# A two-layer attention and retention trunk: transposed halves joined, rotation read from PSUM, outputs kept in the gate tiles, retention scores multiplied earlier

## The chip, the cores and the metric

One core of a Trainium2 chip runs the whole program. The metric is device time in microseconds (us) of one execution, median of the runs. The engines are TensorE (PE, with its weight loads PEld), VectorE (DVE), ScalarE (ACT), GpSimd (POOL) and SyncE (SP), which here issues all DMAs.

## What is computed

The input x has 2048 tokens of 1024 numbers (f32). Two layers follow, and a last RMS norm. Cut to what matters:

```
h    = rms_norm(x, gain)
proj = h @ w_in                      # 1024 -> 8 x 512: aq ak av ag rq rk rv rg
ya   = softmax(aq ak' / 8 + bias[clipped distance]) av      # 8 heads x 64, own chunk of 64 and 8 before
rq, rk = rotary(rq), rotary(rk) * 128 ** -0.5               # 4 heads x 128
yr   = rms_norm(chunkwise retention of rq, rk, rv)          # decay by distance inside a chunk, a state between
y    = concat[ya * silu(ag), yr * silu(rg)]
x    = x + y @ w_out

def apply_rotary(t, cos, sin):
    t1, t2 = split(t, 2)             # halves of 64
    return concat([t1 * c - t2 * s, t1 * s + t2 * c])
```

## The kernel before

**Numbers in two halves.** Every matrix product is made from f16 pairs: a value is split into an upper f16 (`hi`, made by ACT as a rounding copy) and the rest (`lo`, made by DVE as value minus upper), and three products hi*hi, hi*lo, lo*hi are summed in PSUM. So most tiles come as two, `hTh`/`hTl` (normed rows, transposed, one pair for each block of 512 tokens), `whT`/`wlT` (weights), `rh`/`rl` (rows before they are transposed).

**Groups and blocks.** A layer is cut into four groups s (two attention heads and one retention head each), a group into four blocks n of 512 tokens (`NS`), a block into four token tiles a of 128. For each (layer l, group s, block n) there is
- `dense_T`: four projections, j = 0 to 3 (q, k, rotary q, rotary k), with the features on the partitions: 24 matmuls of 512 columns each into a `psD` tile (two buffers), then `evacuate(j)`;
- `dense_V`: four token tiles a, v, rv and both gates, 24 matmuls each into `psD`; then ACT makes v, the gate's Tanh (into `gt`, five buffers) and rv, and `rests` on DVE the low parts;
- `attention`: eight units (a, hx), each with its scores `S` (one PSUM buffer), the exponential, `pq` (upper and rest of the probabilities), a DMA transposition into `pT`, and two units later the product `o` with v; its output, times gate, goes to `ya` and by DMA to `y_d` in DRAM;
- `retention`: for each tile a the scores r1 = rk rq (three products), masked and split into `dT`, and then r2: dT times rv, the state's halves `sh` times rq, and the state's update; its output goes to `yr` and by DMA to `y_d`.

After the last group `wout` loads `y_d` tile by tile, splits, transposes (`y_turn`) and multiplies by w_out; for layer 0 `residual` norms and transposes the new rows.

**What sets the order.** PE, ACT, DVE and POOL run in program order, as written by `run`: in each round one generator step of the dense work (8 matmuls of 512 columns), then `tick()` (what was put off by `later(k, fn)` and is due), then one step of the attention of the block before, then background work from `pull` (weights of the next group, norms). A block is 24 rounds, 12 of `dense_T` and 12 of `dense_V`; an attention unit is 3 rounds, a token tile 6. In round 0 of a tile `next(ret)` issues r1, in round 5 r2; in the very first block (`slow`) r1 and r2 alternate in round 2 of each unit. `later(1..3)` after r1 mask it (DVE, L875), round it (ACT, L860) and make the rest (DVE, L864). SP's order is left to a planner, but for the first block, where it is written by hand.

**The rotation before** (`evacuate`, j = 2 and 3; L662 to L683). ACT copies the PSUM tile to SBUF (`raw`), two DMAs swap its 64-partition halves into `swp`, and then in later rounds DVE multiplies raw by the cosine table `tabc`, swp by the signed sine table `tabs`, and adds; ACT rounds (`upper`), DVE makes the rest (`lower`), ACT a third part, and for k a DMA transposes both halves into `kt`. For q, ACT and DVE make `qq`, and four DMAs (L638) copy its two heads to both halves of the partitions of `st.q`; for k, four DMAs (L649 to L652) place the halves of `kk`. `qq`, `swp`, `tabc`, `tabs` have one buffer each.

The tables of cosine and sine are made on DVE and ACT in the first group (`tables`), stored in DRAM (`tab_d`) and loaded for each block.

Of the kernel before, what the change touches and what calls it, by code (L numbers as in the profile page):

```python
# [13 lines left out]
ALU = mybir.AluOpType  # L14
# [13 lines left out]
def hybrid_trunk(ctx: ExitStack, tc: tile.TileContext, x, pos, gain, gcol, w_in, w_out, rel, fgain,  # L28
# [41 lines left out]
    tab_d = [dp.tile([2, P, 512], F32, tag=f"tab{n}", name=f"tab{n}") for n in range(NS)]  # L70
# [12 lines left out]
    def tables(n, wk):  # L83

        ang, k, r, k2 = wk
# [38 lines left out]
        dve.tensor_scalar(ang, r, -1.0, None, op0=ALU.mult)  # L124
        yield
        for hf in range(2):
            sl = slice(hf * 64, hf * 64 + 64)
            cs = slice(hf * 256, hf * 256 + 256)
            sp.dma_start(tab_d[n][0, 0:64, cs], k2[sl, :])
            sp.dma_start(tab_d[n][0, 64:128, cs], k2[sl, :])  # L130
            sp.dma_start(tab_d[n][1, 0:64, cs], ang[sl, :])
            sp.dma_start(tab_d[n][1, 64:128, cs], r[sl, :])
# [3 lines left out]
    TAB_STEPS = 19  # L136
# [78 lines left out]
    def hT_of(l, n):  # L215
        if (l, n) not in hT:
            hT[l, n] = (hp.tile([P, KT, 512], F16, tag="hTh", name=f"hTh{l}_{n}"),
                        hp.tile([P, KT, 512], F16, tag="hTl", name=f"hTl{l}_{n}"))
        return hT[l, n]

    def row_pair(nm):
        return (b2.tile([P, 1280], F16, tag="sc", name=f"rh{nm}")[:, 0:D],
                b2.tile([P, 1280], F16, tag="pq", name=f"rl{nm}")[:, 0:D])
# [11 lines left out]
    def transpose_rows(rows, dh, dl):  # L235
        sp.dma_start_transpose(out=dh, in_=rows[0])
        sp.dma_start_transpose(out=dl, in_=rows[1])

    class Tok:


        def __init__(self, t, xt, rows):
            self.t, self.x, self.rows, self.nm = t, xt, rows, f"n0_{t}"
            self.hh, self.hl = (h_[:, :, t % 4 * P:(t % 4 + 1) * P] for h_ in hT_of(0, t // 4))
# [21 lines left out]
        def hi(self):  # L266
            if self.rows:
                self.rw = (self.rows[:, 0:D], self.rows[:, D:2 * D])
                act.activation(self.rw[0], self.x, AF.Copy)
                return  # L270
            for h in range(2):
                act.activation(self.hh[:, h * KT // 2:(h + 1) * KT // 2, :], self.pt[h], AF.Copy)

        def lo(self):
            if self.rows:
                dve.tensor_tensor(self.rw[1], self.x, self.rw[0], op=ALU.subtract)
                return
# [4 lines left out]
        def dma(self):  # L282
            transpose_rows(self.rw, self.hh, self.hl)
# [324 lines left out]
    def dense_T(l, s, n, g, st):  # L608
        hh, hl = hT[l, n]
        nm = f"{l}_{s}_{n}"  # L610
        st.tabc = b1.tile([P, 512], F32, tag="tabc", name=f"tabc{nm}")
        st.tabs = b1.tile([P, 512], F32, tag="tabs", name=f"tabs{nm}")
        def tab_load():
            while n not in tab_done:
                pull(1)
            sp.dma_start(st.tabc, tab_d[n][0])
            sp.dma_start(st.tabs, tab_d[n][1])
# [9 lines left out]
        def evacuate(j, ps):  # L627
            if j == 0:
                st.q = b2.tile([P, 2, 2, 512], F16, tag="q", name=f"q{nm}")
                qq = b1.tile([P, 2, 512], F16, tag="qq", name=f"qq{nm}")  # L630
                act.activation(qq[:, 0, :], ps, AF.Copy, scale=2.0 ** -16)

                def q_rest():
                    dve.scalar_tensor_tensor(out=qq[:, 1, :], in0=ps, scalar=2.0 ** -16, in1=qq[:, 0, :], op0=ALU.mult,
                                             op1=ALU.subtract)
                    for hx in range(2):
                        for half in range(2):
                            sp.dma_start(st.q[half * 64:half * 64 + 64, hx], qq[hx * 64:hx * 64 + 64])  # L638

                soon(q_rest)  # L640
            elif j == 1:
                st.k = b3.tile([P, 2, 512], F16, tag="k", name=f"k{nm}")
                kk = b1.tile([P, 2, 512], F16, tag="swp", name=f"kk{nm}")
                kh, kl = kk[:, 0, :], kk[:, 1, :]
                act.activation(kh, ps, AF.Copy, scale=2.0 ** -16)

                def k_rest():
                    dve.scalar_tensor_tensor(out=kl, in0=ps, scalar=2.0 ** -16, in1=kh, op0=ALU.mult, op1=ALU.subtract)
                    sp.dma_start(st.k[0:64, 0, :], kh[0:64, :])  # L649
                    sp.dma_start(st.k[64:128, 1, :], kh[64:128, :])  # L650
                    sp.dma_start(st.k[64:128, 0, :], kl[0:64, :])
                    sp.dma_start(st.k[0:64, 1, :], kl[64:128, :])  # L652

                soon(k_rest)
            else:
                w = 5 - j
                rot = b2.tile([P, w, 512], F16, tag=f"rot{j}", name=f"rot{nm}_{j}")
                if j == 2:
                    raw = rot[:, 1:3].rearrange("p a c -> p (a c)").bitcast(F32)
                else:  # L660
                    raw = b1.tile([P, 512], F32, tag="qq", name=f"raw{nm}")
                act.activation(raw, ps, AF.Copy, scale=2.0 ** -16)  # L662

                def swap(rot=rot, raw=raw, j=j):
                    swp = b1.tile([P, 512], F32, tag="swp", name=f"swp{nm}_{j}")
                    sp.dma_start(swp[0:64, :], raw[64:128, :])
                    sp.dma_start(swp[64:128, :], raw[0:64, :])

                    def turned(out_, x_, y_, op):
                        return lambda: dve.tensor_tensor(out_, x_, y_, op=op)  # L670

                    def upper():
                        act.activation(rot[:, 0], raw, AF.Copy)

                    def lower():
                        dve.tensor_tensor(rot[:, 1], raw, rot[:, 0], op=ALU.subtract)

                    def third():
                        act.activation(rot[:, 2], rot[:, 0], AF.Copy, scale=2.0 ** -11)

                    def tokens():
                        st.kt = b1.tile([P, KT, P], F16, tag="ktok", name=f"kt{nm}")
                        sp.dma_start_transpose(out=st.kt, in_=rot.rearrange("p a c -> p (a c)"))  # L683
# [5 lines left out]
                    later(d + 3, upper)  # L689
                    later(d + 4, lower)  # L690
                    if j == 2:
                        later(d + 5, third)
                    else:
                        later(d + 5 if first else 11, tokens)

                if j == 2:
                    st.rq = rot
                    swap()
                    if first:
                        later(1, tab_load)  # L700
                else:
                    st.rk = rot
                    later(8 if first else 2, swap)
# [34 lines left out]
    def dense_V(l, s, n, g, st):  # L738
        hh, hl = hT[l, n]
# [38 lines left out]
    def attention(l, s, n, g, st, prev):  # L778
# [4 lines left out]
        ya = {}  # L783

        def qk(a, hx):
# [16 lines left out]
            v = b2.tile([P, 640], F32, tag="sc", name=f"sc{u.nm}")[:, 0:w]  # L802
# [5 lines left out]
            pq = b2.tile([P, 1280], F16, tag="pq", name=f"pq{u.nm}")  # L808
# [6 lines left out]
        def pv(u):  # L815
            t = 4 * n + u.a
# [7 lines left out]
            def out_():  # L824
# [3 lines left out]
                if u.hx == 0:  # L828
                    ya[u.a] = b2.tile([P, P], F32, tag="ya", name=f"ya{u.nm}")
                y = ya[u.a]  # L830
                vs = slice(u.hx * 64, u.hx * 64 + 64)
# [7 lines left out]
        ret = retention(l, s, n, g, st)  # L839
        slow = (l, s, n) == (0, 0, 0)  # L840
# [25 lines left out]
    def retention(l, s, n, g, st):  # L866
        for a in range(4):
# [4 lines left out]
            r1 = psR.tile([P, 512], F32, tag="small", name=f"r1{nm}")  # L872
            products(r1[:, 0:P], [(st.rk[:, i, cs], st.rq[:, j, cs]) for i, j in ((0, 0), (0, 1), (1, 0))])
            dT = b1.tile([P, 2, P], F16, tag="dT", name=f"dT{nm}")
            later(1, lambda r1=r1: dve.tensor_tensor(r1[:, P:2 * P], r1[:, 0:P], g.msk, op=ALU.mult))  # L875
            later(2, lambda dT=dT, r1=r1: upper_of(dT, r1[:, P:2 * P]))
            later(3, lambda dT=dT, r1=r1: rest_of(dT, r1[:, P:2 * P]))
            yield
# [32 lines left out]
            def fin(t=t, a=a, r2=r2, ss=ss, nm=nm):  # L911
                y = b1.tile([P, P], F32, tag="yr", name=f"yr{nm}")
                dve.scalar_tensor_tensor(out=y, in0=r2[:, 0:P], scalar=ss[:, 0:1], in1=st.g[a][:, P:256],
                                         op0=ALU.mult, op1=ALU.mult)
# [582 lines left out]
```

## Time and profile before

| | |
|---|---|
| runs, median (lowest to highest) | 2116.13 us (2115.45 to 2116.34), 3 runs |
| profiled execution, span of its instructions | 2120.7 us, 4.6 above the median of the runs |
| ACT and POOL busy in it | 1136.9 us (54%) and 432.8 us (20%) |
| mean granted TensorE clock | 0.987 |
| mean busy share of the 16 DMA engines | 66.4% for SP's queue |

The profiled execution has no time of its own beside its span. A profile's lines name engine, source line (L731 is line 731 of the kernel), operation and tiles as out<-in. "idle before" is the engine's idle time ahead of such instructions, with what ended it. SPq is SP's queue: its entries are the issuing of DMAs. PE's durations overlap one another, since matmuls are pipelined.

### The profile page before, as it was taken

How to read it: one execution, taken by the hardware profiler on the slowest of the kernel's cores; microseconds unless marked ns; L12 is line 12 of the kernel's file. 1: busy time of each engine (PE TensorE's matmuls, PEld its weight loads, DVE VectorE, ACT ScalarE, POOL GpSimd, SP SyncE). 2: the span in 40 equal slices, each digit the busy share in tenths (PEclk: the TensorE clock that was granted, in tenths of full speed). 3: DMA queues.
4: the chain of work that ended last, by engine and by line, in shares of the span. 5: the costliest groups of instructions: out<-in, count | busy, mean ns of one | idle time of the engine just before them, and what ended most of it. 6: DMA issues, size and time to landing. Idle time of an engine off the chain costs nothing.

```text
span 2120.7 us, 39351 instructions
## 1 busy us (share of the span) xinstructions
PE 2014.2 (95%) x14014; PEld 1052.9 (50%) x14014; DVE 1341.8 (63%) x4031; ACT 1136.9 (54%) x2522; POOL 432.8 (20%) x509
## 2 busy tenths in 40 slices
PE   6788999999999999988999999999999999998998
PEld 4334455555555555444444555555555555554543
DVE  7667666666656666566654666566666566666643
ACT  7455565556565554554544546554655665445432
POOL 1112221222122212221000222222222222222200
PEclk9989999999999999999999999999999999999999
DMA  8757675557476765689865556655666866648864
GB/s 247 173 111 162 138 157 119 115 110 156 109 166 133 157 164 100 120 189 254 219 179 123 119 100 135 130 119 100 140 129 123 172 152 157 124 101 176 217 193 127
DMA packets 645702, 313.63 MB, mean 148 GB/s; under 512 B 459233, under 2 KB 602081, under 8 KB 645505
## 3 DMA queue, kind: packets, MB, share of 16 engines
q1 hardware_dynamic: 645504, 311.12, 66.4%
q8 instruction: 109, 1.79, 0.4%
q14 instruction: 89, 0.72, 0.1%
HBM read 123.26 MB, written 41.98 MB: 78 GB/s over the span
## 4 chain that ended last, share of the span: by engine, by line
PE 50%; DMA 8%; DVE 5%; ACT 5%; issue 1%; SPq 1%; POOL 0%; POOLq 0%; DVEq 0%; ACTq 0%
PE dT L731 16%; PE dV L752 15%; PE dO L1093 12%; DMA pT<-pq 3%; PE r L856 2%; PE S L800 2%; PE S L801 2%; DVE sc L804 1%; DMA toep<-rel_d 1%; DMA swp<-rot 1%; PE o L820 1%; ACT pq L809 1%; PE o L821 1%; PE o L822 1%; ACT sc L807 1%
## 5 line engine op out<-in xcount | busy, mean ns | idle before, releaser
L807 ACT ACTIVATE sc<-sc,mq,cT 128x640 f32<-128x640 f32 (+4 forms) x256 | 218.4, 853 | 657.3 <-DVE mq L806 341.5
L810 POOL TENSOR_TENSOR pq<-sc,pq 128x640 f16<-128x640 f32 (+4 forms) x256 | 322.6, 1260 | 1201.7 <-ACT pq L809 610.3
L731 PE MATMUL dT<-hTh,whT 128*128 128x512 f16 x1008 | 350.2, 383 | 13.4 <-DMA hTh<-hTl 9.8
L752 PE MATMUL dV<-whV,hTh 128*128 128x512 f16 x1024 | 355.3, 383 | 4.1 <-DVE gt L770 4.1
L752 PE MATMUL dV<-wlV,hTh 128*128 128x512 f16 x1024 | 353.8, 381 | 0.0
L752 PE MATMUL dV<-whV,hTl 128*128 128x512 f16 x1024 | 353.7, 381 | 0.0
L731 PE MATMUL dT<-hTh,wlT 128*128 128x512 f16 x1008 | 347.0, 379 | 0.0
L731 PE MATMUL dT<-hTl,whT 128*128 128x512 f16 x1008 | 346.8, 379 | 0.0
L752 PEld LDWEIGHTS <-hTh 128*128 128x128 f16 x2048 | 197.5, 99 | 222.9 <-issue 8.2
L731 PEld LDWEIGHTS <-whT 128*128 128x128 f16 x2016 | 192.9, 98 | 225.8 <-issue 23.1
L804 DVE CUSTOM_DVE_ANT_0 sc<-S,bias 128x640 f32<-128x640 f32 (+4 forms) x256 | 188.6, 737 | 79.9 <-PE S L801 69.0
L1093 PE MATMUL dO<-whO,yhy 128*128 128x512 f16 x512 | 195.0, 381 | 1.1 <-DMA yhy<-rhy 1.1
L1093 PE MATMUL dO<-whO,yly 128*128 128x512 f16 x512 | 194.8, 381 | 1.1 <-DMA yly<-rly 1.1
L1093 PE MATMUL dO<-wlO,yhy 128*128 128x512 f16 x512 | 194.6, 380 | 0.0
L809 ACT ACTIVATE pq<-sc 128x640 f16<-128x640 f32 (+4 forms) x256 | 171.5, 670 | 12.5 <-DMA pT<-pq 4.6
L1093 PEld LDWEIGHTS <-yhy 128*128 128x128 f16 x1024 | 100.0, 98 | 116.7 <-DMA yhy<-rhy 1.9
L752 PEld LDWEIGHTS <-hTl 128*128 128x128 f16 x1024 | 99.5, 98 | 110.5 <-issue 2.6
L731 PEld LDWEIGHTS <-wlT 128*128 128x128 f16 x1008 | 97.6, 98 | 109.0 <-issue 1.8
L800 PE MATMUL S<-k,q 128*128 128x128 f16 (+3 forms) x592 | 143.7, 269 | 5.7 <-DVE mq L804 5.6
L820 PE MATMUL o<-v,pT 128*128 128x65 f16 x1120 | 130.2, 194 | 14.6 <-DMA pT<-pq 14.6
L820 PEld LDWEIGHTS <-pT 128*128 128x128 f16 x1120 | 105.6, 97 | 52.5 <-DMA pT<-pq 24.4
L801 PE MATMUL S<-k,q 128*128 128x128 f16 (+3 forms) x592 | 131.2, 270 | 0.0
(350 smaller groups left out, 3354.4 us busy)
## 6 DMA issues: line engine op xcount, KB each, us to landing
q<-qq SPq DMA_DIRECT2D x128, 128.0 KB, 2.5
yyy<-y_d SPq DMA_DIRECT2D x32, 512.0 KB, 4.6
stT<-in_w_in_dram SPq DMA_DIRECT2D x27, 512.0 KB, 5.0
stV<-in_w_in_dram SPq DMA_DIRECT2D x26, 512.0 KB, 4.5
k<-kk SPq DMA_DIRECT2D x128, 64.0 KB, 2.1
swp<-rot SPq DMA_DIRECT2D x64, 128.0 KB, 2.6
tabc<-tab SPq DMA_DIRECT2D x32, 256.0 KB, 2.7
tabs<-tab SPq DMA_DIRECT2D x32, 256.0 KB, 2.8
```

Of the source, the lines that this page charges most:

```text
L731: pe.matmul(ps, w_[:, j, kt, :], h_[:, kt, :], start=(m == 0), stop=(m == 23))
L752: pe.matmul(ps, h_[:, kt, a * P:(a + 1) * P], w_[:, kt, :], start=(m == 0), stop=(m == 23))
L800: pe.matmul(o, st.q[:, hx, 0, cs], k_, start=True, stop=False)
L801: pe.matmul(o, st.q[:, hx, 1, cs], k_, start=False, stop=True)
L804: dve.tensor_tensor_reduce(out=v, in0=S[:, 0:w], in1=g.bias[hx][:, 640 - w:640], scale=1.0, scalar=-3.0e38, op0=ALU.add, op1=ALU.max, accu ...
L807: act.activation(v, v, AF.Exp, bias=m[:, 0:1], scale=g.c[:, 0:1])
L809: act.activation(pq[:, 0:w], v, AF.Copy)
L810: pool.tensor_tensor(pq[:, w:2 * w], v, pq[:, 0:w], op=ALU.subtract)
L820: pe.matmul(o[:, 0:65], u.p[:, b, :], v_[:, 0:65], start=(b == 0), stop=False)
L821: pe.matmul(o[:, 0:64], u.p[:, b, :], v_[:, 65:129], start=False, stop=False)
L856: pe.matmul(out_, w_, m_, start=(i == 0), stop=(i + 1 == len(pairs)))
L1093: pe.matmul(ps, h_[:, kt, :], w_[:, kt, :], start=(m == 0), stop=(m == 23))
```

## The change

- **Halves together.** `hTh` and `hTl` become one tile, and so do the rows' halves and the transposed y; one DMA transposes 2048 columns where two had 1024 each. `sc` (scores, f32) and `pq` become one tile `spq` of two buffers, since the rows' halves lie there. `tabc`/`tabs` become `tab`, `qq`/`swp` become `qk`.
- **Rotation straight from PSUM.** DVE multiplies PSUM by the cosine into `own`, and by the sine, crossing the halves, into `other`: one operation of 64 partitions for each half, reading one half and writing the other. ACT's copies and the swap DMAs go; the sign sits in the scalar, so the table is stored once. q and k are written by ACT and DVE in place, half by half; k needs no DMA, q one for each head.
- **Outputs in the gate tiles.** The products with the gate are written over the gate; when both heads and the retention of a token tile are done (`finished`), one DMA stores the tile.
- **Scores sooner.** r1 and its mask, rounding and rest move to `decayed`, called in round 4 of the tile before (for a block's first tile: in the last tile of the block before; for a layer's first block, 11 rounds after `dense_V` starts). `slow` goes: r2 is issued in round 5 of every tile.

The core of the diff:

```diff
     def transpose_rows(rows, dst):
-        sp.dma_start_transpose(out=dh, in_=rows[0])
-        sp.dma_start_transpose(out=dl, in_=rows[1])
+        sp.dma_start_transpose(out=dst, in_=rows[2])
...
-                qq = b1.tile([P, 2, 512], F16, tag="qq", name=f"qq{nm}")
-                act.activation(qq[:, 0, :], ps, AF.Copy, scale=2.0 ** -16)
+                for hx in range(2):
+                    hs = slice(hx * 64, hx * 64 + 64)
+                    act.activation(st.q[hs, hx, 0], ps[hs], AF.Copy, scale=2.0 ** -16)
                 def q_rest():
-                    dve.scalar_tensor_tensor(out=qq[:, 1, :], in0=ps, scalar=2.0 ** -16, in1=qq[:, 0, :], op0=ALU.mult,
-                                             op1=ALU.subtract)
                     for hx in range(2):
-                        for half in range(2):
-                            sp.dma_start(st.q[half * 64:half * 64 + 64, hx], qq[hx * 64:hx * 64 + 64])
+                        hs, os = slice(hx * 64, hx * 64 + 64), slice(64 - hx * 64, 128 - hx * 64)
+                        dve.scalar_tensor_tensor(out=st.q[hs, hx, 1], in0=ps[hs], scalar=2.0 ** -16, in1=st.q[hs, hx, 0],
+                                                 op0=ALU.mult, op1=ALU.subtract)
+                        sp.dma_start(st.q[os, hx], st.q[hs, hx])
...
                 def k_rest():
-                    dve.scalar_tensor_tensor(out=kl, in0=ps, scalar=2.0 ** -16, in1=kh, op0=ALU.mult, op1=ALU.subtract)
-                    sp.dma_start(st.k[0:64, 0, :], kh[0:64, :])
-                    sp.dma_start(st.k[64:128, 1, :], kh[64:128, :])
-                    sp.dma_start(st.k[64:128, 0, :], kl[0:64, :])
-                    sp.dma_start(st.k[0:64, 1, :], kl[64:128, :])
+                    for hx in range(2):
+                        hs, os = slice(hx * 64, hx * 64 + 64), slice(64 - hx * 64, 128 - hx * 64)
+                        dve.scalar_tensor_tensor(out=st.k[os, hx], in0=ps[hs], scalar=2.0 ** -16, in1=st.k[hs, hx],
+                                                 op0=ALU.mult, op1=ALU.subtract)
...
-                act.activation(raw, ps, AF.Copy, scale=2.0 ** -16)
-                    sp.dma_start(swp[0:64, :], raw[64:128, :])
-                    sp.dma_start(swp[64:128, :], raw[0:64, :])
-                    d = 5 if j == 2 and first else 3
-                    later(d, turned(raw, raw, st.tabc, ALU.mult))
-                    later(d + 1, turned(swp, swp, st.tabs, ALU.mult))
-                    later(d + 2, turned(raw, raw, swp, ALU.add))
...
+                def cosine():
+                    dve.scalar_tensor_tensor(out=own, in0=ps, scalar=2.0 ** -16, in1=st.tab[:, 0], op0=ALU.mult,
+                                             op1=ALU.mult)
+                def sine(half):
+                    i_, o_ = slice((1 - half) * 64, (2 - half) * 64), slice(half * 64, half * 64 + 64)
+                    dve.scalar_tensor_tensor(out=other[o_], in0=ps[i_], scalar=(half * 2 - 1) * 2.0 ** -16, in1=st.tab[i_, 1],
+                                             op0=ALU.mult, op1=ALU.mult)
+                d = 2 * j if first else 1
+                later(d, cosine)
+                later(d, lambda: sine(0))
+                later(d + 1, lambda: sine(1))
+                later(d + 2, lambda: dve.tensor_tensor(own, own, other, op=ALU.add))
...
+        def finished(a):
+            left[a] -= 1
+            if left[a] == 0:
+                t = 4 * n + a
+                sp.dma_start(y_d[t].rearrange("p (a s c) -> p a s c", a=2, c=P)[:, :, s],
+                             st.g[a].rearrange("p (a c) -> p a c", a=2))
...
-                dve.scalar_tensor_tensor(out=y[:, vs], in0=o[:, 0:64], scalar=rl[:, 0:1], in1=st.g[u.a][:, vs],
-                                         op0=ALU.mult, op1=ALU.mult)
-                if u.hx == 1:
-                    sp.dma_start(y_d[t][:, s * P:(s + 1) * P], y)
+                y = st.g[u.a][:, u.hx * 64:u.hx * 64 + 64]
+                dve.scalar_tensor_tensor(out=y, in0=o[:, 0:64], scalar=rl[:, 0:1], in1=y, op0=ALU.mult, op1=ALU.mult)
+                finished(u.a)
...
             u = qk(a, hx)
-            if i % 2 == 0 and not slow:
-                next(ret, None)
-            yield
-            yield
-            if i % 2 == 1 or slow:
+            yield
+            if hx == 1:
+                if a < 3:
+                    decayed(l, s, n, g, st, a + 1)
+                elif nxt is not None:
+                    decayed(*nxt, 0)
+            yield
+            if hx == 1:
                 next(ret, None)
```

More of the change, by code (lines that the diff above doesn't have):

```diff
@@ L696, in evacuate @@
+                rot = b2.tile([P, 5 - j, 512], F16, tag=f"rot{j}", name=f"rot{nm}_{j}")
                 if j == 2:
                     st.rq = rot
-                    swap()
+                    st.tmp = b1.tile([P, 2, 2, 512], F16, tag="qk", name=f"tmp{nm}")
                     if first:
@@ L871, in retention @@
             last = t == NT - 1
[L872 to L877, printed above, removed]
-            yield
+            dT = st.dT
             r2 = psR.tile([P, 512], F32, tag="small", name=f"r2{nm}")
@@ L1261, in hybrid_trunk @@
     sp.dma_start(invf_sb, invf)
-    t0 = tables(0, [gp.tile([P, 256], F32, tag="gt", name=f"wk{i}") for i in range(4)])
+    t0 = tables(0, b2.tile([P, 2560], F16, tag="spq", name="wk").bitcast(F32)[:, 0:1024])
     go_on(t0)
```

174 lines of the change are left out of this document (85 added, 89 removed).

## Prediction

> **What bounds the kernel now.** I read the page's first two lines, then the busy time by stretch, then the list of what the PE waited for, and last the timeline around the longest waits.
>
> ```profile
> span 2120.7 us, 39351 instructions
> ...
> PE 2014.2 (95%) x14014; PEld 1052.9 (50%) x14014; DVE 1341.8 (63%) x4031; ACT 1136.9 (54%) x2522; POOL 432.8 (20%) x509
> ```
>
> The PE is the bound: 2014.2 of 2120.7 us. The change takes no matmul away, so all that it can win lies in the 106.5 us in which the PE stood still, and in slow clock.
>
> ```profile
> 53.00:106.00 53.00, 40.60 (x201) 18.56 (x198) 34.24 (x88) 25.64 (x52) 6.19 (x13) 0.90 0.75 173
> 106.00:212.00 106.00, 86.03 (x565) 43.35 (x566) 75.32 (x205) 57.59 (x123) 22.46 (x25) 0.90 0.67 137
> ...
> 742.00:848.00 106.00, 106.00 (x767) 56.20 (x766) 67.27 (x204) 53.07 (x127) 23.61 (x27) 1.00 0.59 132
> ```
>
> The columns are stretch, length, busy time of PE, weight load, DVE, ACT and POOL, granted clock, DMA share and GB/s. A settled stretch (742 to 848) has no idle PE at full clock: nothing can be won there. From 53 to 212 us 32.4 us are idle and the clock is 0.90. So the question is which waits end last in the disturbed places.
>
> ```profile
> PE r L856 <- DVE dT L864: 20.5, 16, 5.1
> PE o L820 <- DMA pT<-pq: 14.6, 13, 2.4
> PE r L856 <- ACT dT L860: 10.2, 6, 2.9
> PE dT L731 <- DMA hTh<-hTl: 9.8, 1, 9.8
> PE S L800 <- DVE mq L804: 5.6, 2, 2.9
> ...
> PE dV L752 <- DVE gt L770: 4.1, 5, 1.5
> PE dT L731 <- DMA hTh<-rhn: 3.6, 1, 3.6
> ...
> PE r L856 <- DVE sh L864: 2.9, 3, 1.7
> ```
>
> The largest item (total us, times, longest) is the retention's second product, waiting for the decayed scores dT: 20.5 + 10.2 = 30.7 us. Next come the transposed probabilities (14.6) and the first rows of a new 512-token block (9.8 + 3.6). The timeline shows why dT is late at the longest of these waits:
>
> ```profile
> 102.17 1.26 SPq L236 DMA_TRANSPOSE hTh<-rhn  x1
> ...
> 103.62 0.47 SPq L666 DMA_DIRECT2D swp<-rot  x1
> 104.14 0.59 SPq L667 DMA_DIRECT2D swp<-rot  x1
> ...
> 106.76 0.69 DVE L670 TENSOR_TENSOR rot<-rot,tabc 128x512 f32<-128x512 f32 x1 [2.90 <-DMA swp<-rot]
> ...
> 110.09 0.28 DVE L864 SCALAR_TENSOR_TENSOR dT<-dT,r 128x128 f16<-128x128 f16 x1
> ...
> 110.43 0.29 PE L856 MATMUL r<-rv,dT 128*128 128x128 f16 x1 [5.07 <-DVE dT L864]
> ```
>
> Start and length lead each line. SP issued the swap of the rotary halves only at 103.62, behind a transposition; DVE, which takes its work in order, stood 2.90 us for it; everything queued behind, L864 among it, slid, and the PE stood 5.07 us.
>
> **Part 1, scores two rounds sooner.** In the chain that ended last, two equal places of consecutive blocks of the settled part are 52.08 us apart:
>
> ```profile
> 1196.32 5.18 PE dT L731 x24
> ...
> 1248.40 5.18 PE dT L731 x24
> ```
>
> That is 24 rounds of 2.17 us. Before, the scores are multiplied in round 0 of a tile's six rounds, masked, rounded and rested in the ticks of rounds 1, 2, 3, and used in round 5. After, they are multiplied in round 4 of the tile before: the last step falls in round 1, four rounds (8.7 us) ahead of its use instead of two (4.3). In the first block the distance was three rounds from product to use, with the last step in the very round of its use; there it becomes seven. The longest wait is 5.1 us, so 4.3 us more cover nearly every one. What is next late is sh, the halved state, which keeps its three rounds and now is first in line: 2.9 us stay, and some 3 us more that dT's lateness hid (the two are written by the same engines, sh one round earlier). So of 33.6 us (dT and sh) 28 go. Bounds: 15 if half of DVE's lateness reaches sh too, 33 if sh's goes as well. The PE work (three small products a tile) is moved, not added. ACT's rounding into the one dT buffer now comes one round after the previous tile's use instead of three, so ACT may stand up to a round for the PE; what is queued behind it is the next exponential, whose probabilities are used six rounds after their scores, so I cost this at nothing; without that cover it would be 2.17 us a tile on ACT.
>
> **Part 2, rotation from PSUM.** ACT's two copies a block (L662) and four swap DMAs go; DVE gets the sine product in two halves of 64 partitions, each reading one half of the PSUM tile and writing the other half. For q and k, ACT's rounding and DVE's rest become two halves each. The groups by line:
>
> ```profile
> L670 DVE TENSOR_TENSOR swp<-swp,tabs 128x512 f32<-128x512 f32 x64 | 44.0, 687 | 0.1
> ...
> L648 DVE SCALAR_TENSOR_TENSOR kk<-dT,kk 128x512 f16<-128x512 f32 x32 | 22.1, 689 | 39.3 <-ACT kk L645 39.2
> ...
> L662 ACT ACTIVATE raw<-dT 128x512 f32<-128x512 f32 x32 | 18.8, 588 | 9.1 <-PE dT L731 9.1
> L645 ACT ACTIVATE kk<-dT 128x512 f16<-128x512 f32 x32 | 18.8, 587 | 3.9 <-PE dT L731 3.9
> ```
>
> No row has a half-height operation on 512 columns. One end is that it costs as much as a full one (the columns are the same), the other half of it; I take the first. DVE then has four more operations of 0.69 us a block (two sines, one q, one k): 4 x 0.69 x 32 = 88 us, 1342 to 1430, or 67% of the span; at half price 0. ACT loses 2 x 0.588 and gains 2 x 0.587 a block: nothing, or minus 38 at half price. In the settled stretch DVE would go from 67.3 to about 73 of 106 us: still no bound. Against the added busy time stands blocked time that goes, in the list of waits:
>
> ```profile
> DVE rot L670 <- DMA swp<-rot: 60.1, 26, 6.2
> ...
> DVE raw L670 <- DMA swp<-raw: 7.3, 1, 7.3
> ```
>
> 67 us in which DVE held its queue for a swap. The dense PSUM tile (two buffers) is held one round longer, till the second sine; its next writer comes four rounds after, so the PE doesn't see it. The table must be there two rounds sooner; the list of waits names no wait of DVE for it now, but in the first two blocks, where it is made just before, it may hold DVE a us or two (in the +3 below).
>
> The Trainium skill's page "VectorE: DVE Perf Modes" (Rules for kernel authors) speaks against this part: for many operations on a matmul's output it would copy PSUM to SBUF first, and its cost table has 120 fixed cycles from PSUM against 58. By it the three products that read PSUM would cost some 65 ns more each, an estimate of 12 us of DVE in all. The rows above disagree: 689 ns from PSUM, 687 from SBUF.
>
> **Part 3, the DMA queue.** All DMAs are issued by SP, one after the other. The list of issues (count, KB, us to landing), and one line's instructions:
>
> ```profile
> q<-qq SPq DMA_DIRECT2D x128, 128.0 KB, 2.5
> ...
> k<-kk SPq DMA_DIRECT2D x128, 64.0 KB, 2.1
> ...
> y_d<-yr SPq DMA_DIRECT2D x128, 64.0 KB, 2.1
> y_d<-ya SPq DMA_DIRECT2D x128, 64.0 KB, 2.1
> ...
> L812 SPq DMA_TRANSPOSE pT<-pq x256: 1167/1334/3015, 84.7 to 1990.5; - x128
> ...
> L667 SPq DMA_DIRECT2D swp<-rot x32: 581/588/824, 54.6 to 1896.7; - x32
> ```
>
> (The last two rows: issue time in ns, least, median, most.) 64 q copies, all 128 k copies and 128 swaps go: 320 x 0.588 = 188 us of SP. Half of the 256 output DMAs go. Of the 54 pairs of row transpositions 52 become one each. The issue hardly grows with width (1.17 at least, where the first tile's 256 columns are, 1.33 typically, for 1280), so 2048 columns should take about 1.5: 52 x 1.2 = 62 us. Together 250 us, 12% of the span, not counting outputs and tables. Who gains: the probabilities' transpositions queue behind less. Of 14.6 us I take 5 (none to 12).
>
> For the second block's rows the queue alone is the wait (SP's timeline):
>
> ```profile
> 71.42 0.51 SPq L666 DMA_DIRECT2D swp<-raw  x1
> 71.97 0.59 SPq L667 DMA_DIRECT2D swp<-raw  x1
> 72.67 1.56 SPq L236 DMA_TRANSPOSE hTh<-hTl  x1
> 74.32 3.10 SPq L237 DMA_TRANSPOSE hTl<-hTl  x1
> ```
>
> The PE stands 9.8 us till the last of four rows is there; ahead of it SP loses the two swaps above, two more, four of eight table stores and three second transpositions, some 8 us. One transposition of both halves lands later than the first half alone did, so I take 7 (0 to 10). The 3.6 us stay.
>
> **Part 4, outputs in the gate tile.** A tile's two DMAs become one, issued by the last of three writers. The gate tile now is free only when that DMA has landed; ACT's Tanh of the next block (five buffers) waits for it. The last tile's DMA is issued one round before its buffer's Tanh; landing takes 2.1 us, about that round. I put it, the table waits and the joined probability buffer (DVE's first write, not ACT's second, now waits for the transposition of two allocations ago) together at +3 us of PE; bounds -1 and +30.
>
> **Clock.** From 53 to 212 us a clock of 0.90 costs up to 0.10 x 159 = 16 us, next to the idle stretches. With some 25 us of that idle gone I take 6 (0 to 12). The skill's page "TensorE: Matmul & The Clock Gate" (The HAM clock gate) says that the throttled state is the default and activity releases it, at half rate otherwise; the rows agree (0.90 where the PE pauses, 1.00 where it doesn't).
>
> **The sum** against the profiled 2120.7 us: -28 -7 -5 -6 +3 = -43, so 2077.7. The runs' median, 2116.1, is 4.6 below; the same distance gives 2073.
>
> **Rivals.**
> *Half of it comes back (28%).* The scores' lead uncovers sh, and the first stage stays late for its own chain (DVE 75 of 106 us there, rows from DMAs): -15 for dT, nothing for clock, -5 for the rest. 2116 - 20 = 2096.
> *More goes (15%).* The swap stalls were behind sh, the gate rests (4.1) and the S waits (5.6) too, and the queue behind all 14.6 us: -33 -10 -12 -10: 2051.
> *Slower: the gate tile ties ACT to the output DMA (9%).* If SP is late by more than a round, Tanh stands, and the dense PSUM tile behind it is released late. Its next writer comes three rounds (6.5 us) on, so it decides when the DMA lands over 6.5 us after its issue should be. Against it: landing in 2.1 us typically. If every one of the 31 following blocks lost 2.5 us, that is +78 against -43: 2151; the point of no gain is 1.4 us a block.
> *No difference (3%).* SP's order is left to a planner; if it puts the joined DMAs later, the waits move from dT to hT and pT: 2116.
>
> **Numbers.** The forecast, 45%; with the first two rivals faster: 88%, of which 2 go to slower for a case in which unknown costs at their far ends eat the gain. Range 2048 to 2110: it takes in the larger gain and the half that comes back, and leaves out the slower rival and the far ends. Differences below 0.2% (4 us) cannot be told from none. Faster 0.86, same 0.03, slower 0.11.
>
> **What would show it.** Right: the row of r waiting for dT nearly gone; no DVE wait for a swap; PE busy about 2014 and its idle time near 70; DVE about 1430 (1340 would mean that half height costs half); 320 fewer copies and the transposition of 2048 columns issued in about 1.5 us; clock above 0.90 between 53 and 212 us. Wrong: r waiting for sh as it did for dT; a new row of ACT waiting for the output DMA that reaches dV or dT on the PE; SP's issue of the long transpositions at twice 1.3 us; DVE waiting for the table in every block.

## Result and the profile after

The changed kernel takes **2185.01 us** (median of 4 runs, 2182.82 to 2189.24) against 2115.79 (2112.74 to 2116.34) of the kernel before, measured on the same chip: **1.0329 times as long, 95% interval 1.0314 to 1.0343**. It is 69 us slower; the forecast was 43 us faster.

The head of the page of the changed kernel:

```profile
span 2182.5 us, 38458 instructions
...
PE 2030.2 (93%) x14014; PEld 1054.6 (48%) x14014; DVE 1440.9 (66%) x4155; ACT 1148.3 (53%) x2522; POOL 429.4 (20%) x509
```

PE's idle time went from 106.5 to 152.3 us (2182.5 - 2030.2), and its busy time rose by 16 us at the same number of matmuls. The mean clock fell from 0.987 to 0.983; by that alone it would be 8 us (an estimate, 2014.2 x 0.987 / 0.983). Busy time by stretch, with the columns of the prediction's table (stretch, length, PE, weight load, DVE, ACT, POOL, clock, DMA share, GB/s):

```profile
53.00:106.00 53.00, 48.80 (x251) 22.84 (x250) 42.99 (x104) 26.97 (x54) 5.44 (x13) 0.97 0.62 142
106.00:212.00 106.00, 78.79 (x529) 39.73 (x526) 73.81 (x195) 55.20 (x117) 20.99 (x24) 0.92 0.56 119
742.00:848.00 106.00, 104.56 (x751) 55.23 (x752) 78.07 (x218) 53.89 (x127) 23.85 (x30) 1.00 0.51 123
1960.00:2060.00 100.00, 82.36 (x549) 41.86 (x549) 58.82 (x169) 46.18 (x90) 20.80 (x21) 0.90 0.71 162
```

The first 53 us of the disturbed stretch are better than before (PE 48.8 of 53 where it was 40.6). The next 106 are worse (78.8, before 86.0). Together they idle 31.4 us, before 32.4: of the 25 us that were to go here, next to nothing went, though the clock rose as forecast (0.97 and 0.92, before 0.90). The settled stretch has 1.4 us of idle where it had none. And a stretch that the prediction never looked at has become bad: from 1960 to 2060 us, where the last output projection begins while attention still runs, the PE is busy for 82 of 100 us at a clock of 0.90. The kernel before does the same work (found by counting matmuls in both traces) in 78.5 us:

```profile
1919.50:1998.00 78.50, 74.21 (x543) 38.53 (x542) 57.15 (x164) 45.08 (x90) 20.76 (x21) 0.98 0.90 209
```

What the PE waited for in the changed kernel (total us, times, longest), and then the waits of the other engines that are new or larger:

```profile
PE dV L737 <- DVE tmp L671: 21.6, 17, 3.2
PE dV L737 <- DVE gt L755: 16.0, 6, 4.8
PE o L811 <- DMA pT<-spq: 13.2, 11, 2.6
PE msT L322 <- DVE mbT L315: 12.3, 8, 5.5
PE dO L1090 <- DVE gt L755: 9.0, 4, 4.6
PE S L792 <- ACT fj L200: 8.9, 3, 3.4
PE dT L716 <- issue: 5.8, 1, 5.8
...
PE r L844 <- DVE dT L852: 2.1, 2, 1.1
PE r L844 <- DVE sh L852: 1.0, 3, 0.4
...
DVE v L751 <- ACT rv L747: 170.4, 78, 8.2
DVE spq L797 <- DMA pT<-spq: 32.9, 18, 3.7
...
ACT gt L746 <- DMA y_d<-gt: 37.1, 16, 6.3
```

The retention's waits went as forecast: dT from 30.7 to 2.1 us, sh from 2.9 to 1.0. In their place stand waits for the dense PSUM tile: dV waits for the second sine (tmp), and dV and dO for the gate rests (gt), 46.6 us in the three rows (before, dV waited 4.1 for gt). Two waits of other engines are new: DVE for the joined buffer's transposition, and ACT's Tanh for the gate tile's output. One place of the timeline, start and length leading, shows both (SP's queue, ACT, DVE, PE):

```profile
1966.59 3.96 SPq L233 DMA_TRANSPOSE yTy<-rwy  x1
...
1977.97 0.81 SPq L774 DMA_DIRECT2D y_d<-gt  x1
1979.16 3.27 SPq L804 DMA_TRANSPOSE pT<-spq  x1
...
1985.32 0.47 ACT L746 ACTIVATE gt<-dV,ughV 128x256 f32<-128x256 f32 x1 [6.25 <-DMA y_d<-gt]
1986.08 0.29 DVE L751 SCALAR_TENSOR_TENSOR v<-dV,v 128x128 f16<-128x128 f32 x1 [8.16 <-ACT rv L747]
1987.11 0.59 PE L1090 MATMUL dO<-whO,yTy 128*128 128x512 f16 x1 [4.61 <-DVE gt L755]
...
1996.21 0.82 DVE L797 CUSTOM_DVE_ANT_0 spq<-S,bias 128x640 f32<-128x640 f32 x1 [2.20 <-DMA pT<-spq]
```

The output leaves the queue at 1977.97, but the Tanh that reuses its tile is released only at 1985.2: landing took 7.3 us. ACT stands 6.25, DVE 8.16 behind it (it takes its work in order), and the PE 4.61 for the dense PSUM tile. Ten us later DVE's scores stand 2.20 us for a transposition out of the same buffer.

### The profile page after: what moved, and what is told of

Same layout as the page of the kernel before. It is cut to its first block, busy times and chain, and to the rows that moved or that the text cites. A ratio compares the mean times of both kernels' runs of the same rounds, so it can differ in the third digit from the quotient of the medians.

```text
span 2182.5 us, 38458 instructions
## 1 busy us (share of the span) xinstructions
PE 2030.2 (93%) x14014; PEld 1054.6 (48%) x14014; DVE 1440.9 (66%) x4155; ACT 1148.3 (53%) x2522; POOL 429.4 (20%) x509
## 5 line engine op out<-in xcount | busy, mean ns | idle before, releaser
L737 PE MATMUL dV<-whV,hT 128*128 128x512 f16 x2048 | 593.3, 382 | 37.5 <-DVE tmp L671 21.6
L716 PE MATMUL dT<-hT,whT 128*128 128x512 f16 x2016 | 581.9, 383 | 15.9 <-issue 5.8
L800 ACT ACTIVATE spq<-spq,mq,cT 128x640 f32<-128x640 f32 (+4 forms) x256 | 218.6, 854 | 698.4 <-issue 460.4
L802 POOL TENSOR_TENSOR spq<-spq 128x640 f16<-128x640 f32 (+4 forms) x256 | 320.0, 1250 | 1291.4 <-ACT spq L801 670.6
L737 PEld LDWEIGHTS <-hT 128*128 128x128 f16 x3072 | 292.4, 98 | 360.3 <-issue 29.8
L737 PE MATMUL dV<-wlV,hT 128*128 128x512 f16 x1024 | 354.4, 382 | 0.0
L716 PE MATMUL dT<-hT,wlT 128*128 128x512 f16 x1008 | 349.2, 382 | 0.0
L1090 PE MATMUL dO<-whO,yTy 128*128 128x512 f16 x960 | 296.5, 387 | 16.3 <-DVE gt L755 9.0
L797 DVE CUSTOM_DVE_ANT_0 spq<-S,bias 128x640 f32<-128x640 f32 (+4 forms) x256 | 188.2, 735 | 61.6 <-DMA pT<-spq 32.9
L1090 PE MATMUL dO<-wlO,yTy 128*128 128x512 f16 x480 | 185.8, 387 | 1.0 <-DVE wlO L332 1.0
L792 PE MATMUL S<-k,q 128*128 128x128 f16 (+3 forms) x592 | 143.8, 269 | 14.6 <-ACT fj L200 8.9
L811 PE MATMUL o<-v,pT 128*128 128x65 f16 x1120 | 130.4, 194 | 15.1 <-DMA pT<-spq 13.2
```

The costliest lines, as they stand in the source:

```text
L716: pe.matmul(ps, w_[:, j, kt, :], h_[:, kt, :], start=(m == 0), stop=(m == 23))
L737: pe.matmul(ps, h_[:, kt, a * P:(a + 1) * P], w_[:, kt, :], start=(m == 0), stop=(m == 23))
L792: pe.matmul(o, st.q[:, hx, 0, cs], k_, start=True, stop=False)
L797: dve.tensor_tensor_reduce(out=v, in0=S[:, 0:w], in1=g.bias[hx][:, 640 - w:640], scale=1.0, scalar=-3.0e38, op0=ALU.add, op1=ALU.max, accu ...
L800: act.activation(v, v, AF.Exp, bias=m[:, 0:1], scale=g.c[:, 0:1])
L802: pool.tensor_tensor(pq[:, w:2 * w], v, pq[:, 0:w], op=ALU.subtract)
```

## Experiments

The change has four parts: (A) halves in joined tiles, (B) rotation from PSUM with q and k by halves, (C) outputs in the gate tiles, (D) scores sooner. The first four runs undo or mend one part in the changed kernel (2185.0); the second four do one part on the kernel before, or undo A; the last seven test the mechanisms. Ratios are to the kernel before, run on the same chip each time (medians 2117 to 2119 us, where it was 2115.8 beside the changed kernel); so differences between runs of different sessions are uncertain by some 3 us.

| run | median us | ratio, 95% interval |
|---|---|---|
| e1_raw_copy | 2197.9 | 1.0365 (1.0341 to 1.0389) |
| e2_own_out | 2155.4 | 1.0168 (1.0148 to 1.0188) |
| e3_two_transposes | 2182.3 | 1.0294 (1.0274 to 1.0315) |
| e4_scores_late | 2194.0 | 1.0350 (1.0329 to 1.0371) |
| s_B_rotation | 2137.6 | 1.0094 (1.0071 to 1.0116) |
| s_C_gate_tiles | 2138.6 | 1.0095 (1.0071 to 1.0120) |
| s_D_scores_sooner | 2098.5 | 0.9910 (0.9887 to 0.9933) |
| u_A_split | 2149.9 | 1.0142 (1.0113 to 1.0172) |
| c6_gate_tiles_six | 2115.6 | 0.9991 (0.9978 to 1.0005) |
| u_spq_split | 2149.8 | 1.0155 (1.0129 to 1.0180) |
| b_full_height | 2086.8 | 0.9856 (0.9832 to 0.9880) |
| cd6_both | 2100.6 | 0.9922 (0.9896 to 0.9947) |
| m_sine_halves_only | 2116.5 | 0.9998 (0.9989 to 1.0008) |
| md_and_scores | 2100.0 | 0.9919 (0.9904 to 0.9934) |
| bd_no_buffers | 2118.0 | 0.9995 (0.9984 to 1.0007) |

**e1_raw_copy**: the dense PSUM tile is emptied at once by an ACT copy, and DVE turns the copy.

```
+ act.activation(own, ps, AF.Copy, scale=2.0 ** -16)
- cosine, sine: in0=ps
+ cosine, sine: in0=own        # both sines first, then the cosine in place
```

> The changed kernel, but ACT copies the rotary PSUM tiles to SBUF at once (as before the change) and DVE makes both sine halves and the cosine from that copy; the swap DMAs stay away. Theory A (the dense PSUM tile is now given back by DVE's second sine, late in DVE's queue, and the PE waits for it): the row dV waiting for tmp (21.6 us) vanishes and the time falls by 20 to 30 us, to about 2158. Theory B (the gate tile and its output DMA hold ACT, and through it DVE and the PE): little changes here, within 8 us of 2185, and the waits for gt stay near 30 us. Theory C (DVE's 90 us more work are the cost, wherever the operands lie): no change, DVE busy stays near 1440.

It took 13 us more than the changed kernel. The PE's wait for the sine is no longer among the rows, but others grew: of its trace,

```profile
PE o L813 <- DMA pT<-spq: 28.4, 19, 3.2
PE dV L739 <- DVE gt L757: 18.1, 9, 4.8
PE msT L322 <- DVE mbT L315: 14.1, 8, 2.8
```

None of the three theories had a loss; the waits for the gate rests stay, and DVE's busy time does (1437.1 us). So giving the PSUM tile back at once is no remedy: freed by 64 more ACT operations of 0.58 us, the same lateness came out elsewhere. The Trainium skill's page "VectorE: DVE Perf Modes" (Rules for kernel authors), which the prediction weighed, offers copying to SBUF first where many operations follow. Here, with three, that lost, and reading PSUM cost DVE nothing: 688 ns for a sine out of PSUM, 685 to 833 out of SBUF (e1_raw_copy, 64x512 each).

**e2_own_out**: C undone in the changed kernel; outputs go to a tile of their own and by two DMAs as before.

```
- y = st.g[a][:, P:256]                              # gate tile, one DMA by finished(a)
+ y = b1.tile([P, P], F32, tag="yr"); ...            # and "ya" for the two heads, a DMA each
```

> The changed kernel, but outputs go to tiles of their own and by two DMAs a token tile, as before the change. Theory B: ACT's waits of Tanh for the output DMA (37.1 us) vanish, PE's waits for gt fall from 29.6 us (dV 16.0, dO 9.0, dT 4.6) to about 5, time 2155 to 2165. Theory A: the waits for gt fall by less than half, as DVE's gate rests are late for DVE's own queue; time 2178 to 2185. 128 more DMAs on SP cost at most 5 us.

29.6 us less than the changed kernel: the gate tile's output is some 30 of the 69 us. Some 37 remain. ACT's wait for the output is gone, and with it all but 1.2 us of the PE's waits of dO and dT for the gate rests. The largest of the three rows, which were expected at 5 us together, did not fall (it was 16.0), so it has another cause:

```profile
PE dV L737 <- DVE gt L755: 18.8, 8, 4.8
```

Of the 27.4 us between the two traces (2182.5 and 2155.1), 14.4 are idle time of the PE, and 13.0 its busy time (2017.2 us, at a clock of 0.990).

**e3_two_transposes**: each joined transposition of rows issued as two of 1024 columns; the buffers stay joined.

```
- sp.dma_start_transpose(out=dst, in_=rows[2])
+ sp.dma_start_transpose(out=dst[:, 0:KT], in_=rows[0])
+ sp.dma_start_transpose(out=dst[:, KT:2 * KT], in_=rows[1])
```

> The changed kernel, but each pair of row halves is transposed by two DMAs of 1024 columns again (tiles stay joined). Theory D (a joined transposition, issued in 3.06 us at the median where two took 2 x 1.27, blocks SP's queue for those behind it): PE waits for yTy and hT (4.0 + 3.6 and the 6 us at 136 us) shrink, time falls by 8 to 12 us to about 2175. Theories A and B: no change beyond 4 us.

2.7 us less, which is within that uncertainty: the width of the transposition is not where the time went.

**e4_scores_late**: D undone; r1 in round 0 of its own tile again.

> The changed kernel, but the retention's scores are multiplied in round 0 of their own tile again. If moving the scores was a gain, as predicted: the waits of r for dT return at 20 to 35 us and the time rises to about 2210. If it only shifted waits that now stand elsewhere (DVE late everywhere): the time stays within 8 us of 2185, with waits of r in place of waits for tmp and gt.

9 us more than the changed kernel by the medians, between the two expectations; the intervals of the two ratios overlap (1.0329 to 1.0371, 1.0314 to 1.0343). What the PE waits for changed its name for the most part: r waits 42.2 us for dT again, and the three rows that were 46.6 us (tmp, and gt for dV and dO) are 20.3:

```profile
PE r L841 <- DVE dT L849: 34.2, 34, 2.5
...
PE r L841 <- ACT dT L845: 8.0, 7, 2.8
```

**s_B_rotation, s_C_gate_tiles, s_D_scores_sooner**: the kernel before with B, C or D alone (in D's, the very first token tile keeps its place).

> The kernel before with the rotation straight from PSUM alone: no copy of the rotary tiles by ACT, no swap DMAs, q and k in two halves, table in one tile; rows in two transpositions, own output tiles, scores in round 0 as before. With the gate tiles undone some 37 us of the loss stayed. Theory R (the rotation is what costs: the VectorE gets 90 us more work, and the dense PSUM tile waits for its sine): 2135 to 2155 us. Theory J (the joined buffer of scores and probabilities, and the joined rows, are what cost: the VectorE's first write of a unit waits for a transposition): 2105 to 2120 us, the swaps' 67 us of held VectorE being gone.

> The kernel before with the outputs made in the gate tiles alone, one output DMA a tile. If this cost stands by itself (ScalarE's next tanh waits for the output's DMA to land), 2140 to 2150 us, as undoing it won 30 us in the changed kernel. If it needs the SyncE queue's longer transpositions to become late, within 10 us of before: 2113 to 2126 us.

> The kernel before with the retention's scores of a token tile taken two rounds sooner alone (in the first block the first tile's stay where they were). Prediction's part 1: the 33.6 us of waits for the decayed scores and the state go to 6, 2085 to 2095 us. Undoing it in the changed kernel cost 9 us only: if the waits only change their name, 2105 to 2112 us.

B alone costs 20.6 us, C alone 21.7, and D alone gains 18.5. D lies between the two expectations. Its waits of the PE:

```profile
PE dV L761 <- DVE gt L779: 12.2, 6, 4.9
...
PE r L868 <- DVE sh L876: 3.5, 4, 2.2
...
PE r L868 <- DVE dT L876: 2.1, 2, 1.2
```

The 33.6 us of waits for dT and sh fell to 5.6, the 28 of the forecast. But the wait for the gate rests rose from 4.1 to 12.2; the longest, 4.9 us, ends at 128 us, where before r waited for dT (at 126.6 and 128.3). I read this as DVE's queue being as late as before, and its next customer paying. In C's trace ACT's new wait stands:

```profile
ACT gt L770 <- DMA y_d<-gt: 42.5, 24, 6.3
```

**u_A_split**: the changed kernel with A undone: `sc` and `pq`, `hTh` and `hTl` apart, two transpositions. **u_spq_split**: the same, but the transposed hidden rows stay in one tile; it differs from e3_two_transposes in the joined buffer alone.

```
- spq = b2.tile([P, 2560], F16, tag="spq"); v, pq = spq[:, 0:1280].bitcast(F32)[:, 0:w], spq[:, 1280:2560]
+ v = b2.tile([P, 640], F32, tag="sc")[:, 0:w]
  ...                                                 # exponential
+ pq = b2.tile([P, 1280], F16, tag="pq")
```

> The changed kernel with the halves apart again: scores and probabilities in a tile each, rows' halves in a tile each and two transpositions, two tiles of transposed hidden rows. Theory J (joined buffers cost some 35 us): 2145 to 2155 us. Theory R: 2175 to 2190 us, no more than the 3 us of the two transpositions.

> The changed kernel with scores and probabilities, and the rows' halves, in a tile each again (and so two transpositions), the transposed hidden rows still in one tile. It differs from e3_two_transposes (2182 us) only in that the joined buffer is apart. If the joined buffer makes the loss (the VectorE's scores wait till the probabilities' transposition has landed): 2148 to 2156 us, as u_A_split. If the joined tile of hidden rows makes it: 2175 to 2185 us.

Both are 35 us faster than the changed kernel and equal to each other: of A, it is the joined buffer. The joined buffer holds scores with probabilities, and the two halves of rows; these were not tried apart. In u_spq_split DVE's scores wait for the PE's S (and 2.3 us for y rows):

```profile
DVE sc L799 <- PE S L796: 19.1, 30, 1.5
```

The row with 32.9 us for `pT<-spq` is gone. In the kernel before, the scores' tile was free as soon as POOL had made the rest of the probabilities; joined, it is free only when the transposition has landed, and then DVE, with everything queued behind it, stands. Counted at the same matmul in both traces, the changed kernel is 3 us behind u_A_split at 900 us, 16 behind at 1040, 14 at 1930, and 35 at 2061: the loss falls where output projection and attention run together and the y rows go through the same two buffers. There, too, lie 16 of the 18 waits of the row. The transpositions that they wait for landed 3.3 to 5.1 us after their issue, 3.4 being the median of all. The stretch at the last projection, in u_A_split:

```profile
1946.00:2046.00 100.00, 93.34 (x636) 47.45 (x635) 65.03 (x178) 51.73 (x99) 21.87 (x23) 1.00 0.84 199
```

**c6_gate_tiles_six**: C alone on the kernel before, with six gate tiles. **cd6_both**: that with D.

```
- gt = gp.tile([P, 256], F32, tag="gt")               # five
+ gt = gp.tile([P, 256], F32, tag="gt", bufs=6)
```

> The kernel before with the outputs made in the gate tiles, as in s_C_gate_tiles (2138.6 us), but six gate tiles in place of five, so that ScalarE's tanh comes to a tile three rounds later. Theory W (the tanh waits for the tile's output to land, and with it the VectorE and the PE): most of the 22 us comes back, 2117 to 2125 us, and the 42.5 us of ScalarE's waits for the output fall below 10. If the one output DMA in place of two, or its place in the queue, is what costs: 2132 to 2140 us.

> The kernel before with the scores sooner and the outputs in six gate tiles. If six tiles take the wait away and the parts add up: 2098 to 2106 us, no better than the scores alone (2098.5 us). A gain over them, to 2090 us, would need the output's second DMA to cost the queue something.

The whole cost of C went with one more tile: 2115.6 us, within the measurement of the kernel before. ACT's wait for the output is gone, and DVE's wait for ACT's rv falls from the first row (five tiles) to the second (six), which is what the kernel before has (108.3):

```profile
DVE v L775 <- ACT rv L771: 139.1, 64, 7.1
```

```profile
DVE v L775 <- ACT rv L771: 108.5, 68, 4.3
```

So one output DMA in place of two brings nothing that shows, and cd6_both equals D alone. Six tiles in the changed kernel itself were not tried.

**b_full_height** and **m_sine_halves_only**: B alone on the kernel before, without the doubling of any operation, and with that of the sine only. b_full_height leaves out the crossing of the halves, so it computes something else; its DMAs are those of s_B_rotation in number and size, and it is there for its time alone.

```
- sine(0), sine(1): 64 partitions each                # q, k: ACT and DVE by halves
+ sine: other = ps * tab, 128 partitions              # q, k: one operation each        (b_full_height)

- q, k by halves
+ q, k as before the change, spread by DMA            # sine stays in two halves        (m_sine_halves_only)
```

> s_B_rotation (2137.6 us) with its half-height operations made full-height: one sine, one rounding and one rest for q and for k, so the halves are not turned and the outputs' values are others. VectorE has four operations of 0.69 us a block less (88 us in all), ScalarE two less; PSUM is still read by the rotation. If the number of operations costs: 2098 to 2118 us. If the PSUM tile that waits for the rotation costs: 2130 to 2138 us.

> s_B_rotation (2137.6 us) with q and k made as before (one rounding, one rest, the halves spread by DMA), the rotation still straight from PSUM with its sine in two halves: two of the four added VectorE operations a block stay. b_full_height, without any of the four, took 2086.8 us. If each added operation costs alike: about 2112 us. If it is the sine's halves, which also hold the PSUM tile: 2128 to 2138 us. If it is q's and k's: 2087 to 2100 us.

Without the four added DVE operations a block (and two of ACT's) B is a gain: 2086.8 us, 31 below the kernel before and 51 below s_B_rotation. With the sine's two halves, but q and k whole, it is 2116.5, 30 above the one and 21 below the other. These two steps are not clean prices: with q and k whole, six more copies a block come back, and `other` shares a buffer with k's parts, for which DVE waits:

```profile
DVE oth L676 <- DMA k<-kk: 10.7, 8, 3.5
```

The waits of the PE, first of s_B_rotation, then of b_full_height:

```profile
PE r L845 <- DVE dT L853: 25.1, 33, 2.5
PE o L810 <- DMA pT<-pq: 20.2, 12, 2.7
PE dV L743 <- DVE tmp L677: 11.4, 18, 1.9
PE msT L328 <- DVE mbT L321: 8.5, 8, 2.0
PE dV L743 <- DVE gt L761: 7.3, 5, 2.7
```

```profile
PE o L801 <- DMA pT<-pq: 17.5, 16, 2.3
PE r L836 <- DVE dT L844: 12.1, 12, 2.5
PE dV L734 <- DVE gt L752: 5.7, 5, 2.9
...
PE msT L328 <- DVE mbT L321: 3.1, 3, 1.7
...
PE dV L734 <- DVE tmp L669: 1.1, 2, 0.9
```

The rows in which the PE waits for DVE shrink together, from 79.2 to 42.0 us in all (for ACT from 8.2 to 6.7, for DMAs from 24.6 to 23.2), and the sine's nearly goes although the sine still reads PSUM. So what costs is a longer queue of DVE, not one particular hold. ACT's two operations a block were not tried apart from DVE's four.

**md_and_scores** and **bd_no_buffers**: D with m_sine_halves_only; B and D without A and C.

> m_sine_halves_only with the scores two rounds sooner, which took 18.5 us off the kernel before: if the parts add up, 18 us below m_sine_halves_only, about 2094 us by the first theory there, against 2098.5 us of the scores alone.

> The changed kernel with the joined buffers and the gate-tile outputs undone: the rotation and the sooner scores alone on the kernel before. If the four parts add up (+20.6 for the rotation, -18.5 for the scores): 2116 to 2121 us. If the rotation costs more once the scores no longer wait (the PE then waits for the dense tile instead): 2125 to 2140 us.

B and D together take 2118.0 us: the +20.6 and the -18.5 add up. From there C costs 31.9 (u_A_split, 2149.9), A 37.4 (e2_own_out, 2155.4), and both 67.0 (2185.0), the sum of the two to some 2 us. md_and_scores, 2100.0, gains nothing over D alone. **Of the versions that turn the halves, D alone is the fastest**, 2098.5 us against 2117 of the kernel before; cd6_both and md_and_scores are level with it.

## Why the prediction was wrong, point by point

Two steps failed: that DVE is no bound and its added work therefore free (part 2), and the +3 us for the gate tile and the joined buffer (part 4). A third, the queue's relief, happened and was worth little.

- **Part 1 (scores sooner, -28).** The mechanism is right: the waits for dT and sh fell by 28 us. The term is too large, 18.5 measured alone: 8.1 us of it came back at the gate rests (the sum had named only sh as next late). In the changed kernel it is 9 us or less (e4_scores_late).
- **Part 2 (rotation, nothing on the PE).** The sizes were right: a half-height operation costs a full one, 128 of them 88.1 us, and DVE's busy time became 1440.9 (forecast 1430):

```profile
L671 DVE SCALAR_TENSOR_TENSOR tmp<-dT,tab 64x512 f32<-64x512 f32 x128 | 88.1, 688 | 1.9
```

  The failed step is "its next writer comes four rounds after, so the PE doesn't see it", with "still no bound" for DVE at 73 of 106 us (it became 78). The writer comes three rounds after the tile is complete, as the prediction itself says among its rivals: in the trace 6.0 to 6.7 us in most blocks. In the 62 rotary tiles after the first block the second sine ended 2.9 to 11.9 us after the tile was complete; in half of them the writer started 0.65 us or less after it, and 17 times the PE waited (21.6 us in all). After 300 us the longer of these waits come back in the first block of a group, while DVE still splits weights: from 736 to 750 us two operations of 1.28 us for that (L332) stand among the rotation's. So DVE, at 66% on average, is late in bursts, and each added operation delays dT, the gate rests and the dense tile at once. Doubling the operations cost 51 us of time for 88 us of DVE (and 38 of ACT). What B takes away (ACT's copies, the swaps and the waits for them, the copies of q and k) was worth more than the forecast's balance of nothing too (b_full_height, -31), so the part is -31 + 51 = +20.
- **Part 3 (the queue, -12).** The relief came: the issues took 1118 us of SP before and 840 after, 278 less (forecast 250, without outputs and tables). What it was worth did not. The second block's wait for its rows is gone (9.8 us), but the third block's first matmul now waits 5.8, till 141.94 us, for its last rows, whose joined transposition landed at 141.85; the 3.6 stayed, and the probabilities' waits went from 14.6 to 13.2: some 5 us instead of 12. The 2048 columns were issued in 1.9 us (hidden rows) and 3.06 (y rows) typically, not 1.5, so the rows' transpositions together gave back 23 us of SP (168 to 145), not 62.
- **Part 4 (gate tile, tables, joined buffer: +3, bounds -1 to +30).** This is the term that failed most. Measured are some 30 us for the gate tile and 35 for the joined buffer, in the changed kernel. The prediction named both mechanisms. The gate tile it priced by the typical landing: a store lands 2.2 us after its issue at the median, but up to 7.3. In 16 of 31 blocks ACT's last Tanh waited, 37.1 us in all, and seven of these waits (2.4 to 6.3 us) make 30.7 of them: before five of them the store took 2.9 to 7.3 us to land, and before the other two it was issued 2.6 and 3.0 us after the last write to a gate tile. The joined buffer had no price of its own; there landings were typical, and the cost came in the two stretches with the y rows. No table wait of DVE appeared.
- **Clock (-6).** From 53 to 212 us it rose as forecast, but the idle time there did not go, and elsewhere it fell: 0.90 at the last projection.
- **The sum.** Alone or undone the parts measure -18.5 (D), +20.6 (B), +30 (C) and +35 (A), 67 in all against 69 of the whole.
- **The rivals.** The slower one had the right mechanism for 30 us, at 9%. Its sign, a landing over 6.5 us after the issue should be, is met clearly once, at 1985 us; waits below it already cost. It was the only way to a slower kernel that was worked out, so the joined buffer's and DVE's prices, each as large, were not in it.

What stays open: the joined buffer alone on the kernel before was not tried. How far the PE's slower work, and not the waits themselves, makes up each part was not separated: of the 61.8 us between the two profiled executions 45.8 are idle time and 16.0 busy time.

## What to carry to other kernels

A buffer's lifetime ends with its slowest reader. So joining two tiles, or sending a DMA out of a tile that a compute engine must refill, makes an engine wait for a DMA's landing; price that by the longest landing and the latest issue in the busiest stretch, and try one more buffer first (on the kernel before, one more gate tile took the whole 22 us away). An engine that is busy for two thirds of the span and feeds the bound in order is not free: here 51 us of time for 128 added DVE operations of 0.69 us (with 64 of ACT), although the settled stretch before showed a PE without idle time. Try the parts of a change one by one: here one gained 18.5 us while three lost it four times over.

## What was not expected of the hardware

The transposition of both halves, 2048 columns, in the changed kernel, and the two of 1024 columns each in the kernel before (issue time in ns: least, median, most):

```profile
L233 SPq DMA_TRANSPOSE yTy<-rwy x30: 1707/3059/5984, 907.7 to 2146.5; - x30
L233 SPq DMA_TRANSPOSE hT<-rwn x14: 1318/1912/4607, 99.4 to 1159.3; - x14
```

```profile
L236 SPq DMA_TRANSPOSE yhy<-rhy x32: 1232/1252/2179, 883.0 to 2091.2; - x32
L237 SPq DMA_TRANSPOSE yly<-rly x32: 1231/1282/2634, 890.0 to 2094.7; - x32
```

One of 2048 columns of y rows holds SP for 3.06 us typically and up to 6, two of 1024 for 2.53 together; of hidden rows, one takes 1.91. Over all rows of the changed kernel, joined transpositions took 145 us of SP and pairs (e3_two_transposes) 157: joining saves little of the queue. And a DVE operation on 64 partitions takes as long as on 128 (688 and 683 to 689 ns for 512 columns), whether it reads PSUM or, in most cases here, SBUF (685 ns; one form in e1_raw_copy took 833).
